# Gate operands by pairs of tokens, and one product for eight tokens, in a one-core two-block kernel

## The chip, the cores and the metric

The kernel runs on one core of one Trainium2 chip, in one launch. The metric is device time in microseconds (us): the time of one execution on the chip. The time before is the median of three runs.

## What is computed

The reference is a model of two blocks on 256 tokens of width 1024. The first mixes three branches (a gated linear recurrence, a stick-breaking attention and an attention to a memory) and ends in a convolved feed-forward layer. The second mixes an attention with another recurrence and ends in a layer of 16384 experts. Only this last layer concerns the change:

```python
s = jnp.einsum('thcd,hcnd->thcn', qp, subkeys)        # 8 heads, 2 x 128 keys
v1, i1 = lax.top_k(s[:, :, 0], 16)
v2, i2 = lax.top_k(s[:, :, 1], 16)
...                                                   # the best 16 of the 16 x 16 sums, per head
eidx = jnp.take_along_axis(cidx, p, axis=-1)          # expert = i1 * 128 + i2
gates = jax.nn.softmax(sc, axis=-1)
ue, ve = u[eidx], v[eidx]
act = jax.nn.gelu(jnp.einsum('td,thkd->thk', xb, ue), approximate=False)
return jnp.einsum('thk,thkd->td', gates * act, ve)
```

So each token picks 128 experts (8 heads by 16), with a gate each; the output sums gate times gelu(x u) times v over them.

## The kernel before, in words

The kernel gathers nothing. It multiplies all tokens by all 16384 rows of u, takes the gelu, multiplies the result by a dense matrix of gates that is zero where an expert was not picked, and multiplies that by all of v. Expert number i1 * 128 + i2 has i1 on the 128 partitions and i2 along the free axis. The activations are two buffers `act` (A[0] and A[1], one for each half of i2), each 128 partitions by 64 values of i2 by 256 tokens, the token innermost, float32.

**The stages of `peer` (line 1682).** `peer_select` (line 1582) finds the picked experts, with some tiles of the u product between its steps; it leaves four fp16 tiles `ix`: i1, i2, and the gate times 16384 as a high and a low part, 128 slots on the partitions and 256 tokens along the free axis. Then lines 1749 to 1754 write down: the rest of the u product, `gate(0)`, `values(0)`, `gate(1)`, `values(1)`. A tile of the u product is 48 matmuls of 256 columns into PSUM tile `psg` (float32 split into a high and a low part, weights `whi` and `wlo`), then a gelu into `act`. `values` multiplies a half of the activations (again split, tiles `hn`) by v into four PSUM tiles `out`, 24 matmuls of 512 columns for each of 32 steps. For both products ScalarE makes `whi` and VectorE makes `wlo` of each load `wraw`.

**`gate(half)` (line 1697)** takes eight tokens at a time (G = 8), 32 times. VectorE compares i1 with 0 to 127 into `oa` (line 1707), i2 with this half's 64 values into `ob` (line 1710), and multiplies `ob` by the two parts of the gate into `oc` (line 1713). All three are fp16 with four tokens innermost; `iof` (line 1685) holds each of 0 to 127 four times, so that both operands are read in runs of four. Then, for each of two groups of four tokens, TensorE multiplies each token's `oa` (128 slots by 128 values of i1, the weights) by its `oc` (128 slots by 2 x 64, the moving operand) into a quarter of a PSUM tile `g` (line 1718). Both operands are read with a step of four elements, 8 bytes. The 128 columns of a token are the high and the low part of the gates of 64 experts. ScalarE takes the low part into `gs` (line 1723), VectorE adds the high part to it (line 1724, here the sum), and VectorE multiplies the four tokens' columns of the activations by it (line 1726, here the product). In PSUM and in `gs` the 64 experts are innermost, in `act` the tokens; the product reads `gs` with the token as its inner index, one float every 256 bytes.

**What orders the work.** The kernel writes its operations into a list, and a planner (`Program.run`, line 347) replays them with costs of its own (line 560 for matmuls: 0.061 us for a g matmul; line 594 for VectorE) and puts them in the order of their planned starts, on all engines. A buffer of a tag is free again when its last use has ended in this replay. In this part TensorE takes the ready matmul with the longest work behind it. So the interleaving of g with psg and out is fixed when the kernel is built, and each engine follows its own fixed list. The tags here are `oa`, `ob`, `oc` with two buffers each (lines 1841 to 1843) and `gs` with three (line 1844); two PSUM tiles are left for `g`. Every instruction is issued from line 514, which is why the profile's rows all name it; the tiles tell them apart.

Of the kernel before, what the change touches and what calls it, by code (L numbers as in the profile page):

```python
# [12 lines left out]
F16 = mybir.dt.float16  # L13
U32 = mybir.dt.uint32
AF = mybir.ActivationFunctionType
ALU = mybir.AluOpType
# [3 lines left out]
P = 128  # L20
T = 256
# [130 lines left out]
class View:  # L152
# [15 lines left out]
    v = rearrange  # L168
# [348 lines left out]
class Kernel:  # L517
# [67 lines left out]
    def act(self, out, in_, func=AF.Copy, bias=None, scale=None, accum_out=None):  # L585
        kw = {}
        for k, x in (("bias", bias), ("scale", scale), ("accum_out", accum_out)):
            if x is not None:
                kw[k] = x
        cost = 0.094 + out.n * 0.83e-3 + 0.093 * sum(isinstance(x, View) for x in (bias, scale))  # L590
        o = self.pr.op("ACT", "activation", (out, in_, func), kw, [in_, bias, scale], [out, accum_out], cost)
        o.table = TABLE.get(func)
# [1089 lines left out]
    def peer(self, outs, H, Q0):  # L1682
        pr, act = self.pr, self.act
        hh, hl = self.ktiles(H[:2]), self.ktiles(H[2:])
        iof = pr.buf("iof", 4 * P, F16)
        self.copy(iof.rearrange("p (n t) -> p n t", t=4),
                  self.iota.rearrange("p (n u) -> p n u", u=1).to_broadcast([P, P, 4]))
        A = [pr.buf("act", 64 * T) for _ in range(2)]

        def done(i, ps):  # L1690
            if i == 0:
                self.first_u = ps
            act(A[i // 32][:, (i % 32) * 512:(i % 32) * 512 + 512], ps, AF.Gelu)

        ix = self.peer_select(hh, hl, A[1], Q0, lambda i, j: self.gemm_t("u", range(i, j), hh, hl, done))

        def gate(half):
            a3 = A[half].rearrange("p (n t) -> p n t", t=T)
            G = 8
            for q in range(T // G):  # L1700
                ts_ = slice(q * G, q * G + G)

                tok = lambda v, n: v[:, ts_].rearrange("p (g u t) -> p g u t", u=1, t=4).to_broadcast([P, 2, n, 4])
                four = lambda o: o.rearrange("p (g n t) -> p g n t", g=2, t=4)
                rep = lambda v: v.rearrange("p (u n t) -> p u n t", u=1, t=4)
                oa = pr.buf("oa", G * P, F16)
                self.tt(four(oa), tok(ix[0], P), rep(iof).to_broadcast([P, 2, P, 4]), ALU.is_equal)

                eq, hl = pr.buf("ob", G * 64, F16), pr.buf("oc", G * P, F16)
                self.tt(four(eq), tok(ix[1], 64), rep(iof[:, half * 256:half * 256 + 256]).to_broadcast([P, 2, 64, 4]),  # L1710
                        ALU.is_equal)
                for n in range(2):
                    self.mul(four(hl[:, n * G * 64:(n + 1) * G * 64]), four(eq), tok(ix[2 + n], 64))
                oa3, hl3 = four(oa), hl.rearrange("p (u g n t) -> p u g n t", u=2, g=2, t=4)
                for g in range(2):
                    ps = self.ps("g")
                    for t in range(4):
                        self.mm(ps[:, t * P:(t + 1) * P].rearrange("p (u n) -> p u n", u=2), oa3[:, g, :, t],
                                hl3[:, :, g, :, t])
                    pv = ps.rearrange("p (t u n) -> p u t n", t=4, u=2)  # L1720
                    sm = pr.buf("gs", T)
                    s3 = sm.rearrange("p (t n) -> p t n", t=4)
                    act(s3, pv[:, 1], scale=1.0 / 16384)
                    self.stt(s3, pv[:, 0], 1.0 / 16384, s3, ALU.mult, ALU.add)
                    av = a3[:, :, q * G + g * 4:q * G + g * 4 + 4]
                    self.mul(av, av, sm.rearrange("p (t n) -> p n t", t=4))

        def values(half):
            for i in range(half * 32, half * 32 + 32):
                vs = self.weights("v", i)  # L1730
                hl = pr.buf("hn", 1024, F32R)
                hi, lo = hl[:, :512], hl[:, 512:]
                self.split(A[half][:, (i % 32) * 512:(i % 32) * 512 + 512], hi, lo)
                order = [(j, tb, hf) for j in range(2) for tb in range(2) for hf in range(2)]
                for j, tb, hf in order if i < 63 else sorted(order, key=lambda x: x[1:]):
                    wh, wl = vs[j]
                    s = slice(j * T + tb * P, j * T + tb * P + P)
                    last = i == 63 and j == 1
                    o = outs[tb * 2 + hf]
                    w = slice(hf * 512, hf * 512 + 512)  # L1740
                    for n, (l, r) in enumerate(((hi, wh), (hi, wl), (lo, wh))):
                        self.mm(o, l[:, s], r[:, w], False, last and n == 2, skip=True)
                if i == 62:

                    ss = self.small(1)
                    o = self.pr.op("ACT", "activation", (ss, self.eps, AF.Sqrt), {}, [self.eps, hi], [ss], 0.1)
                    o.table = TABLE[AF.Sqrt]

        self.gemm_t("u", range(24, 32), hh, hl, done)
        self.gemm_t("u", range(32, 64), hh, hl, done)  # L1750
        gate(0)
        values(0)
        gate(1)
        values(1)

        gb = A[0][:, 0:1024]
        self.load(gb, self.a["normf_g"].partition_broadcast(P))
        sq = A[0][:, 3072:3584]
        for tb in range(2):
            ss, y = self.small(2), A[0][:, (tb + 1) * 1024:(tb + 2) * 1024]  # L1760
            hs = [slice(half * 512, half * 512 + 512) for half in range(2)]
            for half, h in enumerate(hs):
                act(sq, outs[tb * 2 + half], AF.Square, accum_out=ss[:, half:half + 1])
            self.add(ss[:, 0:1], ss[:, 0:1], ss[:, 1:2])
            act(ss[:, 0:1], ss[:, 0:1], AF.Sqrt, scale=1.0 / 1024, bias=self.eps)
            for half, h in enumerate(hs):
                self.mul(y[:, h], outs[tb * 2 + half], gb[:, h])
            self.recip(ss[:, 0:1], ss[:, 0:1])
            act(y[:, hs[0]], y[:, hs[0]], scale=ss[:, 0:1])
            self.ts(y[:, hs[1]], y[:, hs[1]], ss[:, 0:1], ALU.mult)  # L1770
            for h in hs:
                self.store(self.o["out"][tb * P:(tb + 1) * P, h], y[:, h])
# [6 lines left out]
    def run(self):  # L1779
# [3 lines left out]
        with ExitStack() as ctx:  # L1783
# [42 lines left out]
            with tc.tile_pool(name="ap", bufs=1) as ap:  # L1826
                for name, n in (("act", 2), ("ix", 4), ("iof", 1), ("oa", NOA), ("ob", NOB), ("oc", NOC), ("gs", NGS)):
                    pr.tag(name, ap, n)
# [12 lines left out]
NOA = 2  # L1841
NOB = 2
NOC = 2
NGS = 3
NQ0 = 2
RE = (0, 0, 0, 0, 0)
NEARLY = 1
# [99 lines left out]
```

## Time and profile before

| | us |
|---|---|
| median of 3 runs | 1532.84 |
| lowest, highest | 1531.59, 1533.38 |
| the profiled execution | 1533.29 |
| its span, first to last instruction | 1531.5 |

The profile is of one execution. Its span is 1.8 us shorter than its time; the rest lies around the first and the last instruction. A busy time is the union of an engine's records; a record's length includes the way through the engine, so records of one engine overlap, and the distance from one start to the next is what an instruction costs in a row of them. Loads of weights into TensorE have an engine of their own (PEld), since they overlap the matmuls (PE). The first block ends near 545 us (the last matmul of its feed-forward layer on gh starts at 544.9), the product w_q begins at 686.9, the last step of the choice of experts (tile ig) ends by 941.3, and from there to the end run the rest of the u product, the gates and the v product.

### The profile page before, as it was taken

To read this page: it belongs to the slowest core of one execution; us is meant where nothing else is said; L and a number is where in the kernel's file an instruction comes from. 1 tells how busy PE (TensorE), PEld (TensorE's weight loads), DVE (VectorE), ACT (ScalarE), POOL (GpSimd) and SP (SyncE) were. 2 spreads that over 40 slices of the span, in tenths; PEclk is the share of its full clock that TensorE was granted. 3 is DMA by queue.
4 is the path that set the end of the run, shared out by engine and by line. 5 is a ranking of instruction groups with operands and counts; after the bars stand their busy time and mean duration, and the time that the engine had idled before them with its cause. 6 is when DMAs were issued, how large, how long until landed. Compare 5 with 4: busy or idle time off the path is not lost.

```text
span 1531.5 us, 28738 instructions
## 1 busy us (share of the span) xinstructions
PE 1507.1 (98%) x11828; PEld 1384.5 (90%) x11828; DVE 1206.9 (79%) x2214; ACT 821.3 (54%) x1169; POOL 41.0 (3%) x52
## 2 busy tenths in 40 slices
PE   7999999999999999999999999999999999999998
PEld 7888889999999999799999999999997777788886
DVE  7895585678888569767977899999969999955554
ACT  5663575446666465664444446555555555544444
POOL 0010000000123000000000000000000000000000
PEclk9999999999999999999999999999999999999999
DMA  6432124555455553334454555343454444455553
GB/s 234 163 111 85 61 79 138 193 195 184 175 191 187 174 207 119 138 122 182 168 191 175 184 174 185 140 163 138 163 179 169 161 160 157 159 193 192 191 192 135
DMA packets 38436, 249.09 MB, mean 163 GB/s; under 512 B 4000, under 2 KB 7456, under 8 KB 9504
## 3 DMA queue, kind: packets, MB, share of 16 engines
q1 hardware_dynamic: 38304, 247.26, 45.2%
q8 instruction: 92, 1.51, 0.4%
q14 instruction: 40, 0.33, 0.1%
HBM read 246.19 MB, written 1.05 MB: 161 GB/s over the span
## 4 chain that ended last, share of the span: by engine, by line
PE 92%; DVE 4%; ACT 2%; DMA 1%; issue 1%; SPq 0%; ACTq 0%; DVEq 0%
PE psg L514 57%; PE out L514 22%; PE ps L514 8%; PE g L514 4%; DVE wlo L514 2%; ACT whi L514 1%; PE sc L514 0%; DMA wraw<-in_w_rwkv 0%; DMA wraw<-in_w_up 0%; DVE tmp L514 0%; ACT mo L514 0%; ACT L514 0%; DVE gate L514 0%; PE hs L514 0%; ACT act L514 0%
## 5 line engine op out<-in xcount | busy, mean ns | idle before, releaser
L514 ACT ACTIVATE whi<-wraw 128x1024 fp32r<-128x1024 f32 (+1 forms) x458 | 482.3, 1055 | 526.3 <-PE psg L514 336.0
L514 DVE TENSOR_TENSOR wlo<-wraw,whi 128x1024 fp32r<-128x1024 f32 (+1 forms) x458 | 559.7, 1225 | 233.9 <-ACT whi L514 231.1
L514 PE MATMUL psg<-hn,whi 128*128 128x256 f32 x3808 | 692.8, 284 | 10.3 <-ACT whi L514 8.9
L514 PEld LDWEIGHTS psg<-hn,whi 128*128 128x128 f32 x3808 | 589.9, 190 | 11.4 <-ACT whi L514 8.9
L514 PE MATMUL psg<-hn,wlo 128*128 128x256 f32 x1904 | 538.1, 283 | 1.3 <-DVE wlo L514 1.3
L514 PEld LDWEIGHTS psg<-hn,wlo 128*128 128x128 f32 x1904 | 360.5, 189 | 2.2 <-DVE wlo L514 2.2
L514 PE MATMUL out<-whi,hn 128*128 128x512 f32 x1024 | 332.0, 396 | 0.0
L514 PEld LDWEIGHTS out<-whi,hn 128*128 128x128 f32 x1024 | 193.4, 189 | 40.4
L514 PE MATMUL out<-wlo,hn 128*128 128x512 f32 x512 | 200.7, 392 | 0.0
L514 PEld LDWEIGHTS out<-wlo,hn 128*128 128x128 f32 x512 | 96.6, 189 | 18.5
L514 ACT ACTIVATE gs<-g 128x256 f32<-128x256 f32 x128 | 49.1, 383 | 73.8 <-PE g L514 53.2
L514 PE MATMUL g<-oc,oa 128*128 128x128 f16 x512 | 80.2, 295 | 0.2 <-DVE gs L514 0.2
L514 DVE TENSOR_TENSOR act<-act,gs 128x256 f32<-128x256 f32 x128 | 80.0, 626 | 0.0
L514 PE MATMUL psg<-whi,hn 128*128 128x512 f32 x224 | 77.2, 405 | 0.3 <-ACT rg L514 0.3
L514 PEld LDWEIGHTS <-oa 128*128 128x128 f16 x512 | 45.6, 120 | 18.9 <-DVE act L514 7.7
L514 DVE SCALAR_TENSOR_TENSOR gs<-g,gs 128x256 f32<-128x256 f32 x128 | 53.8, 420 | 0.1
L514 PEld LDWEIGHTS psg<-whi,hn 128*128 128x128 f32 x224 | 42.1, 188 | 11.2 <-issue 1.2
L514 DVE TENSOR_TENSOR oc<-ob,ix 128x512 f16<-128x512 f16 x128 | 50.3, 421 | 0.0
L514 PE MATMUL psg<-gh,wlo 128*128 128x256 f32 x176 | 49.7, 283 | 0.6 <-DVE wlo L514 0.6
L514 PE MATMUL psg<-gl,whi 128*128 128x256 f32 x176 | 49.6, 282 | 0.0
L514 PE MATMUL psg<-gh,whi 128*128 128x256 f32 x176 | 49.5, 281 | 0.0
L514 PE MATMUL psg<-yh,wlo 128*128 128x256 f32 x160 | 45.2, 282 | 0.0
(319 smaller groups left out, 1756.2 us busy)
## 6 DMA issues: line engine op xcount, KB each, us to landing
wraw<-in_u SPq DMA_DIRECT2D x64, 1024.0 KB, 4.8
wraw<-in_v SPq DMA_DIRECT2D x64, 1024.0 KB, 4.8
wraw<-in_w_up SPq DMA_DIRECT2D x22, 1024.0 KB, 4.8
wraw<-in_w_gate SPq DMA_DIRECT2D x12, 1024.0 KB, 4.8
wraw<-in_w_out SPq DMA_DIRECT2D x8, 1024.0 KB, 5.0
wraw<-in_w_down SPq DMA_DIRECT2D x8, 1024.0 KB, 4.8
wraw<-in_w_q SPq DMA_DIRECT2D x8, 1024.0 KB, 4.9
wraw<-in_w_rwkv SPq DMA_DIRECT2D x6, 1024.0 KB, 4.9
```

The costliest lines, as they stand in the source:

```text
L514: getattr(eng[e], method)(*[lower(x) for x in args], **{k: lower(x) for k, x in kw.items()})
```

## The change

Tokens lie two by two innermost in the fp16 operands: `iof` holds each number twice, the views of `oa`, `ob` and `oc` have four groups of two tokens, and a matmul reads its operands with a step of two elements. `gs` becomes a buffer of 64 experts by eight tokens, the token innermost. The activation and the sum of each group of four tokens read PSUM with the token as the inner index, one float every 512 bytes, and write their four tokens' columns of that buffer. One product of 512 elements for eight tokens follows both groups, with `gs` read in its own order. `gs` has two buffers in place of three.

```diff
-        iof = pr.buf("iof", 4 * P, F16)
-        self.copy(iof.rearrange("p (n t) -> p n t", t=4),
-                  self.iota.rearrange("p (n u) -> p n u", u=1).to_broadcast([P, P, 4]))
+        iof = pr.buf("iof", 2 * P, F16)
+        self.copy(iof.rearrange("p (n t) -> p n t", t=2),
+                  self.iota.rearrange("p (n u) -> p n u", u=1).to_broadcast([P, P, 2]))
...
-                tok = lambda v, n: v[:, ts_].rearrange("p (g u t) -> p g u t", u=1, t=4).to_broadcast([P, 2, n, 4])
-                four = lambda o: o.rearrange("p (g n t) -> p g n t", g=2, t=4)
-                rep = lambda v: v.rearrange("p (u n t) -> p u n t", u=1, t=4)
+                tok = lambda v, n: v[:, ts_].rearrange("p (g u t) -> p g u t", u=1, t=2).to_broadcast([P, 4, n, 2])
+                four = lambda o: o.rearrange("p (g n t) -> p g n t", g=4, t=2)
+                rep = lambda v: v.rearrange("p (u n t) -> p u n t", u=1, t=2)
                 oa = pr.buf("oa", G * P, F16)
-                self.tt(four(oa), tok(ix[0], P), rep(iof).to_broadcast([P, 2, P, 4]), ALU.is_equal)
+                self.tt(four(oa), tok(ix[0], P), rep(iof).to_broadcast([P, 4, P, 2]), ALU.is_equal)
...
-                oa3, hl3 = four(oa), hl.rearrange("p (u g n t) -> p u g n t", u=2, g=2, t=4)
+                oa3, hl3 = four(oa), hl.rearrange("p (u g n t) -> p u g n t", u=2, g=4, t=2)
+                sm = pr.buf("gs", G * 64).rearrange("p (n t) -> p n t", t=G)
                 for g in range(2):
                     ps = self.ps("g")
                     for t in range(4):
-                        self.mm(ps[:, t * P:(t + 1) * P].rearrange("p (u n) -> p u n", u=2), oa3[:, g, :, t],
-                                hl3[:, :, g, :, t])
-                    pv = ps.rearrange("p (t u n) -> p u t n", t=4, u=2)
-                    sm = pr.buf("gs", T)
-                    s3 = sm.rearrange("p (t n) -> p t n", t=4)
-                    act(s3, pv[:, 1], scale=1.0 / 16384)
-                    self.stt(s3, pv[:, 0], 1.0 / 16384, s3, ALU.mult, ALU.add)
-                    av = a3[:, :, q * G + g * 4:q * G + g * 4 + 4]
-                    self.mul(av, av, sm.rearrange("p (t n) -> p n t", t=4))
+                        j = g * 4 + t
+                        self.mm(ps[:, t * P:(t + 1) * P].rearrange("p (u n) -> p u n", u=2), oa3[:, j // 2, :, j % 2],
+                                hl3[:, :, j // 2, :, j % 2])
+                    pv = ps.rearrange("p (t u n) -> p u n t", t=4, u=2)
+                    s4 = sm[:, :, g * 4:g * 4 + 4]
+                    act(s4, pv[:, 1], scale=1.0 / 16384)
+                    self.stt(s4, pv[:, 0], 1.0 / 16384, s4, ALU.mult, ALU.add)
+                self.mul(a3[:, :, ts_], a3[:, :, ts_], sm)
...
-NGS = 3
+NGS = 2
```

The comparison into `ob` changes in the same way as the one into `oa`.

## Rows read from the trace of the kernel before

**Rows 1.** The page: TensorE's busy time with its share of the span and its instructions, and the chain that ended last, by engine.

```profile
PE 1507.1 (98%) x11828; PEld 1384.5 (90%) x11828; DVE 1206.9 (79%) x2214; ACT 821.3 (54%) x1169; POOL 41.0 (3%) x52
PE 92%; DVE 4%; ACT 2%; DMA 1%; issue 1%; SPq 0%; ACTq 0%; DVEq 0%
```

**Rows 2.** Busy time by stretch: the stretch in us, its length, then busy us and number of instructions of PE, PEld, DVE, ACT and POOL, the granted TensorE clock, the DMA engines' busy share and GB/s.

```profile
946.70:1106.20 159.50, 159.50 (x1342) 156.75 (x1341) 157.45 (x294) 82.09 (x132) 0.00 (x0) 1.00 0.42 152
1106.20:1143.90 37.70, 37.70 (x320) 37.50 (x319) 24.50 (x37) 18.10 (x24) 0.00 (x0) 1.00 0.48 168
1143.90:1331.40 187.50, 187.34 (x927) 147.11 (x925) 183.40 (x319) 99.89 (x149) 0.00 (x0) 1.00 0.46 166
1331.40:1531.50 200.10, 193.60 (x849) 158.58 (x847) 109.64 (x117) 95.26 (x116) 0.00 (x0) 0.99 0.50 179
```

**Rows 3.** The same stretches for the instructions that write or read tile g alone: PE (the g matmuls), PEld, DVE (the sums), ACT.

```profile
946.70:1106.20 159.50, 39.51 (x256) 0.00 (x0) 26.50 (x63) 24.20 (x64) 1.00 0.42 152
1106.20:1143.90 37.70, 3.03 (x20) 0.00 (x0) 1.69 (x4) 1.41 (x4) 1.00 0.48 168
1143.90:1331.40 187.50, 36.98 (x232) 0.00 (x0) 24.73 (x59) 23.00 (x60) 1.00 0.46 166
1331.40:1531.50 200.10, 0.64 (x4) 0.00 (x0) 0.83 (x2) 0.45 (x2) 0.99 0.50 179
```

**Rows 4.** The last stretch for tile out: PE (matmuls, two of them begun before the stretch), PEld (their weight loads), DVE, ACT.

```profile
1331.40:1531.50 200.10, 193.37 (x845) 158.23 (x843) 2.77 (x4) 2.72 (x8) 0.99 0.50 179
```

**Rows 5.** The timeline of PE around one group of g in the u stretch: start, us from the first start to the last end of the merged instructions, engine, line, operation, out<-in, shape, count.

```profile
954.40 0.64 PE L514 MATMUL g<-oc,oa 128*128 128x128 f16 x4
954.79 0.49 PE L514 MATMUL psg<-hn,whi 128*128 128x256 f32 x2
955.12 0.28 PE L514 MATMUL psg<-hn,wlo 128*128 128x256 f32 x1
955.24 0.40 PE L514 MATMUL psg<-hn,whi 128*128 128x256 f32 x2
955.48 0.28 PE L514 MATMUL psg<-hn,wlo 128*128 128x256 f32 x1
```

**Rows 6.** The timeline of PEld at the same group, the weight loads of g.

```profile
954.40 0.35 PEld L514 LDWEIGHTS <-oa 128*128 128x128 f16 x4
```

**Rows 7.** The timeline of PE around one group of g in the v stretch.

```profile
1201.52 0.64 PE L514 MATMUL g<-oc,oa 128*128 128x128 f16 x4
1201.91 0.48 PE L514 MATMUL out<-whi,hn 128*128 128x512 f32 x1
1202.23 0.39 PE L514 MATMUL out<-wlo,hn 128*128 128x512 f32 x1
1202.45 0.63 PE L514 MATMUL out<-whi,hn 128*128 128x512 f32 x2
1202.92 0.39 PE L514 MATMUL out<-wlo,hn 128*128 128x512 f32 x1
```

**Rows 8.** The timeline of DVE in the v stretch: a sum, a product and the split of weights behind it.

```profile
1206.44 0.42 DVE L514 SCALAR_TENSOR_TENSOR gs<-g,gs 128x256 f32<-128x256 f32 x1
1206.78 0.63 DVE L514 TENSOR_TENSOR act<-act,gs 128x256 f32<-128x256 f32 x1
1207.32 1.22 DVE L514 TENSOR_TENSOR wlo<-wraw,whi 128x1024 fp32r<-128x1024 f32 x1
```

**Rows 9.** Groups of instructions of DVE, and one of ACT, by operation, tiles and shape: out<-in, shapes, count | busy us, mean ns of one | idle us before, what ended it.

```profile
L514 DVE TENSOR_TENSOR act<-act,gs 128x256 f32<-128x256 f32 x128 | 80.0, 626 | 0.0
L514 DVE SCALAR_TENSOR_TENSOR gs<-g,gs 128x256 f32<-128x256 f32 x128 | 53.8, 420 | 0.1
L514 DVE TENSOR_TENSOR act<-act 128x256 f32<-128x256 f32 x48 | 18.0, 420 | 0.0
L514 DVE TENSOR_TENSOR hn<-act,hn 128x512 fp32r<-128x512 f32 x64 | 43.7, 685 | 0.0
L514 DVE TENSOR_TENSOR kt<-dd,rq 128x512 f32<-128x512 f32 x3 | 2.1, 697 | 0.0
L514 DVE TENSOR_TENSOR oc<-ob,ix 128x512 f16<-128x512 f16 x128 | 50.3, 421 | 0.0
L514 DVE TENSOR_TENSOR oa<-ix,iof 128x1024 f16<-128x1024 f16 x64 | 44.0, 687 | 0.0
L514 ACT ACTIVATE gs<-g 128x256 f32<-128x256 f32 x128 | 49.1, 383 | 73.8 <-PE g L514 53.2 <-DVE act L514 18.9 <-DVE wlo L514 1.1
```

**Rows 10.** The page's costliest groups, matmuls and weight loads, with the same columns.

```profile
L514 PE MATMUL psg<-hn,whi 128*128 128x256 f32 x3808 | 692.8, 284 | 10.3 <-ACT whi L514 8.9
L514 PE MATMUL g<-oc,oa 128*128 128x128 f16 x512 | 80.2, 295 | 0.2 <-DVE gs L514 0.2
L514 PEld LDWEIGHTS psg<-hn,whi 128*128 128x128 f32 x3808 | 589.9, 190 | 11.4 <-ACT whi L514 8.9
L514 PEld LDWEIGHTS <-oa 128*128 128x128 f16 x512 | 45.6, 120 | 18.9 <-DVE act L514 7.7
```

**Rows 11.** Who waited for whom from 946 to 1335 us: the waiting instruction, what ended the wait, us in all, times, the longest.

```profile
ACT gs L514 <- PE g L514: 53.2, 91, 1.4
ACT gs L514 <- DVE act L514: 18.9, 17, 1.9
```

More of the change, by code (lines that the diff above doesn't have):

```diff
@@ L1701, in gate @@
                 ts_ = slice(q * G, q * G + G)
-                tok = lambda v, n: v[:, ts_].rearrange("p (g u t) -> p g u t", u=1, t=4).to_broadcast([P, 2, n, 4])
-                four = lambda o: o.rearrange("p (g n t) -> p g n t", g=2, t=4)
-                rep = lambda v: v.rearrange("p (u n t) -> p u n t", u=1, t=4)
+                tok = lambda v, n: v[:, ts_].rearrange("p (g u t) -> p g u t", u=1, t=2).to_broadcast([P, 4, n, 2])
+                four = lambda o: o.rearrange("p (g n t) -> p g n t", g=4, t=2)
+                rep = lambda v: v.rearrange("p (u n t) -> p u n t", u=1, t=2)
                 oa = pr.buf("oa", G * P, F16)
-                self.tt(four(oa), tok(ix[0], P), rep(iof).to_broadcast([P, 2, P, 4]), ALU.is_equal)
+                self.tt(four(oa), tok(ix[0], P), rep(iof).to_broadcast([P, 4, P, 2]), ALU.is_equal)
                 eq, hl = pr.buf("ob", G * 64, F16), pr.buf("oc", G * P, F16)
-                self.tt(four(eq), tok(ix[1], 64), rep(iof[:, half * 256:half * 256 + 256]).to_broadcast([P, 2, 64, 4]),
+                self.tt(four(eq), tok(ix[1], 64), rep(iof[:, half * P:half * P + P]).to_broadcast([P, 4, 64, 2]),
                         ALU.is_equal)
```

## The prediction

> **What bounds the kernel now.** I read the page's busy times and its chain first, then busy times by stage, then single instructions of the gate stages. TensorE is busy for 98% of the span, and 92% of the chain that ended last lies on it [rows 1]. The granted clock is 1.00 in all the stages that matter, the 2.4 GHz level [rows 2]. So a change pays only where TensorE has less to do, or where another engine begins to hold it up.
>
> The change touches the gate work, the tile g. Its 512 matmuls lie mainly in two stretches [rows 3]: in the first (946.7 to 1106.2 us, half 0) they are strewn among the matmuls of the table u, in the second (1143.9 to 1331.4 us, half 1) among those of v. TensorE is full in both, and VectorE nearly so: 157.45 of 159.50 us and 183.40 of 187.50 us [rows 2]. Between and after them TensorE is full and VectorE has room.
>
> I divide by the work on eight tokens, a portion of eight g matmuls: 256/8 = 32 portions in the first stretch, 232/8 = 29 in the second [rows 3]. A portion takes 159.5/32 = 4.98 us in half 0, with VectorE busy for 4.92 of it, and 187.5/29 = 6.47 us in half 1, with VectorE busy for 6.32. The two engines are within 0.06 and 0.15 us of each other: what one saves counts only as far as the other follows. At the end of half 1, 843 matmuls of v are left (by their weight loads [rows 4]), where the second half alone has 768; so the gate work is 75 matmuls early, 17 us at 0.23 us each.
>
> **TensorE's part.** In the u stretch the three psg matmuls from 955.12 to 955.48 us take 0.12 us each. Four g matmuls and two of psg lie from 954.40 to 955.12, so the four take 0.72 - 0.24 = 0.48 us, 0.12 each [rows 5]. In the v stretch four g and one out take 0.71 us from 1201.52 on, and an out takes 0.23: again 0.48 [rows 7]. A g matmul streams 128 columns, one of psg 256, one of out 512. From 256 to 512 columns the price goes from 0.12 to 0.23 us, 0.43 ns a column; 128 columns should take 0.12 - 0.055 = **0.065 us**. The g matmuls cost almost twice that, the price of 256 columns, and their records are longer too (295 ns against 284 [rows 10]). What sets them apart is the step: their fp16 operands are read every 8 bytes, those of psg and out every 4. The change makes it 4. The bounds are thus 0.065 and 0.120 us. I take 0.065: the rows with a step of 4 bytes stream at that rate and hide a weight load of 128 columns behind every matmul, though their load records are the longer ones (190 ns against 120 [rows 10]). That takes 8 x 0.055 = 0.44 us off a portion, so TensorE would need 4.54 us in half 0 and 6.03 in half 1.
>
> The counts of matmuls and weight loads stay, and so do the bytes of the DMAs; no DMA is moved.
>
> **VectorE's part.** Consecutive instructions overlap, so I take start to start: 0.34 us for a sum (record 420 ns), 0.54 us for a product with the activations (626 ns) [rows 8, 9].
>
> - The product: two of 256 elements go (1.08 us), one of 512 comes. A plain product of 256 takes 420 ns; the present one takes 206 more [rows 9]. It reads runs of four activations and, as second operand, one float of gs every 256 bytes. Products on stepped runs in an earlier part (kt<-dd,rq: runs of 16, 4 and 1 floats) show 697 ns for 512 elements, hardly over the 685 of contiguous ones (hn<-act,hn) [rows 9]; so I blame gs, which becomes contiguous. Bounds: 685 ns, or 685 + 412 = 1097 with the surcharge kept on all 512 elements. I take 690, start to start 0.60. Saved: 0.48 us.
> - The sums (two a portion) now read PSUM one float every 512 bytes, where before they read runs of 64. No row shows such a read. The stepped SBUF read above is nearest by its step (+206 ns), the present sum by its memory (+0). I take the middle, +103 ns, and keep both ends. A gain I exclude: the sum's 420 ns are what a plain SBUF product of 256 pays [rows 9]. Added: 0.21 us.
> - The fp16 preparation (ob, oa, two oc) has the same elements in runs of two in place of four. 512 fp16 elements take 421 ns, 512 fp32 ones 685 [rows 9], so two go at a time, and two is what a run still holds. I take no change; at one at a time ob, oc and oa would cost 0.27 x 3 + 0.54 = 1.3 us more a portion.
> - The copy that makes iof halves, once, long before the gates: nothing.
>
> VectorE has 0.48 - 0.21 = 0.27 us less to do: 4.65 us a portion in half 0, 6.05 in half 1. At the ends of the sum's price it is 4.44 and 5.84, or 4.86 and 6.26.
>
> **ScalarE and buffers.** The activation that begins each sum reads the same PSUM shape in 383 ns [rows 9]; the same surcharge (0 to 206 ns) adds at most 0.41 us a portion. ScalarE is busy 82.09 of 159.50 and 99.89 of 187.50 us [rows 2], which covers it; without that cover it would hold the sums in VectorE's queue for as long. It waits 53.2 us for g and 18.9 for act [rows 11]. The sums of eight tokens now wait in one buffer for a later product, but two buffers hold sixteen tokens where three held twelve, so the wait on act should shrink. Behind the product in VectorE's queue stands the split of the next weights, wlo, which TensorE needs next; it moves by 0.1 us at most.
>
> **The sum.** TensorE needs 4.54 and 6.03 us, VectorE 4.65 and 6.05. VectorE would set the pace, and since it never was fuller than 98.7%, I add 1%: 4.70 and 6.11. Half 0: (4.98 - 4.70) x 32 = 9.0 us. Half 1: (6.47 - 6.11) x 29 = 10.4 us. The 24 g matmuls outside [rows 3]: 1.3 us. Less 1 us for what the planner may lose in a new order: **19.7 us**. The profiled execution took 1533.3 us, 0.45 above the median of the runs; 1533.3 - 19.7 = 1513.6, **1514 us**. At the sum's lower end TensorE paces and all 0.44 us count: 14.1 + 12.8 + 1.3 = 28.2 us, 1505. At its upper end VectorE needs 4.91 and 6.32: 2.2 + 4.4 + 1.3 = 7.9 us, 1525.
>
> **Rivals.**
>
> *The g matmuls stay at 0.12 us.* The f32 weight load hides behind a matmul of 0.12; the g load need not hide behind one of 0.065. If a load of 0.055 us and a stream of 0.065 go one after the other, that is 0.12 with any step. For it: the four loads of a group follow one another without a break, 0.35 us from 954.40 on [rows 6]. Against it: no other matmul in these rows works in such turns. VectorE's savings are then hidden: 1533 us, within 3. The Trainium skill speaks for this one. Its page "TensorE: Matmul & The Clock Gate", section "LDWEIGHTS (loading the stationary operand)", counts a load by its columns, P/1.2 ns, 107 ns for 128; and "SBUF — State Buffer", section "Door 1: The DMA port swizzle", asks for two hits on each 16-byte line, which a step of 8 bytes already gives. By these rules the step would not matter and the time would stay; the load record of 120 ns agrees with the first, the 190 ns of as many f32 columns does not.
>
> *VectorE sets a slower pace: slower than before.* Its place is the sums' PSUM read. If one float per 512 bytes takes twice the time per element, a sum goes from 420 to the 685 ns of 512 elements, +0.53 us a portion; and if the product's surcharge comes from the activations' runs, 1 KB apart, and not from gs, it takes 1097 ns, 1.01 start to start, and saves only 0.07. VectorE: +0.46, 5.38 and 6.78 us; (5.38 - 4.98) x 32 + (6.78 - 6.47) x 29 = 12.8 + 9.0 = 22 us more, 1555. It decides once both sums' surcharges and the product come to over 1.08 + 0.06 = 1.14 us; then no faster matmul helps. The kt rows speak against the product's half; nothing speaks for or against the sums'. The skill's "PSUM — Partial Sum Buffer", section "Specifications (TRN2)", has lines of 8 bytes and says that non-contiguous patterns slow matmuls; no row here shows what they do to a reader.
>
> *In between*: the stream gets faster but the load shows, 0.09 us a matmul. TensorE: 4.74 and 6.23 us; 7.7 + 7.0 + 0.7 = 15 us less, 1518.
>
> **How the numbers follow.** Matmuls at the new price and VectorE within its bounds: 0.50 (1505 to 1526). In between: 0.08. Matmuls unchanged: 0.26 (1530 to 1536). VectorE slower: 0.16 (1537 to 1555; a small surcharge is likelier than both large ones). So faster by over 0.2% (3 us, about what a measurement of this kernel can tell from no change) has 0.58, within it 0.26, slower 0.16. The range from 1503 to 1538 leaves out most of the slow case and a little below.
>
> **What the new profile would show.** Right: g matmuls 60 to 70 ns apart; a product of 512 elements near 690 ns; sums between 420 and 626 ns; VectorE at 99% in both stretches if they are dear, TensorE full if not. Wrong: g still 0.12 us apart (then 1533), or products over 1 us or sums over 690 ns with TensorE waiting for VectorE's oc or gs (then above 1537).

## The result, and the profile after

The changed kernel takes **1507.62 us** (median of 4 runs, 1506.92 to 1508.46); the kernel before takes 1533.11 beside it (4 runs). The ratio is 0.9835, interval 0.9823 to 0.9847: 25.5 us less. The forecast was 1514, 6.4 us too slow. The profiled execution took 1508.46 us, with a span of 1506.7.

The page's busy time and its chain by engine, which answer to [rows 1]:

```profile
PE 1482.4 (98%) x11828; PEld 1361.0 (90%) x11828; DVE 1176.2 (78%) x2150; ACT 813.0 (54%) x1169; POOL 41.0 (3%) x52
PE 93%; DVE 4%; ACT 2%; issue 1%; DMA 1%; SPq 0%; DVEq 0%; ACTq 0%
```

TensorE is still the engine that the end hangs on; it has 24.7 us less to do, almost the whole gain. The stages, which answer to [rows 2] (PE, PEld, DVE, ACT, POOL, granted clock, DMA share, GB/s); they now end at the last g matmul of the u stretch (280 of the 512 are done by then), the end of the u product, the last g matmul of all, and the span's end:

```profile
947.50:1105.50 158.00, 158.00 (x1454) 156.23 (x1454) 155.35 (x290) 86.31 (x142) 0.00 (x0) 1.00 0.46 166
1105.50:1129.90 24.40, 24.40 (x210) 24.40 (x209) 11.12 (x10) 11.57 (x14) 0.00 (x0) 1.00 0.49 173
1129.90:1310.50 180.60, 180.60 (x942) 139.77 (x941) 170.62 (x290) 95.13 (x150) 0.00 (x0) 1.00 0.49 177
1310.50:1506.70 196.20, 189.67 (x832) 155.41 (x829) 107.20 (x112) 93.92 (x114) 0.00 (x0) 0.99 0.49 178
```

TensorE is full in both gate stretches, at the same granted clock of 1.00. VectorE, forecast as the new bound at 99%, stands at 98.3% (155.35 of 158.00) and 94.5% (170.62 of 180.60). The last psg matmul starts at 1129.87 us instead of 1143.76: 13.9 us of the gain lie ahead of it, the rest behind it.

Now TensorE's timeline around a group of g in the u and in the v stretch, as in [rows 5, 7] (start, us, instruction, count):

```profile
1105.35 0.28 PE L514 MATMUL psg<-hn,wlo 128*128 128x256 f32 x1
1105.47 0.40 PE L514 MATMUL g<-oc,oa 128*128 128x128 f16 x4
1105.68 0.48 PE L514 MATMUL psg<-hn,whi 128*128 128x256 f32 x2
1106.00 0.28 PE L514 MATMUL psg<-hn,wlo 128*128 128x256 f32 x1
...
1310.32 0.40 PE L514 MATMUL g<-oc,oa 128*128 128x128 f16 x4
1310.53 0.47 PE L514 MATMUL out<-whi,hn 128*128 128x512 f32 x1
1310.85 0.40 PE L514 MATMUL out<-wlo,hn 128*128 128x512 f32 x1
```

Four g matmuls and two of psg take 0.53 us, where they took 0.72: less 0.24 for psg, 0.29 are left for the four. In the v stretch it is 0.53 less 0.23, 0.30. Within the group the matmuls are quicker: from the first start to the last end there are 0.40 us, less one record of 0.22, so three steps of 0.06 (start to start the median is 58 ns, where it was 118). The fourth step gains far less. From the start of a group's last g matmul to the second f32 matmul behind it the median over the trace is 0.228 us with psg and 0.341 with out, where it was 0.251 and 0.364: 0.023 us less, not 0.060. The second out comes 0.32 us after the first, as it did before [rows 7]; a last g matmul of 58 ns fills less of that time than one of 118. TensorE's weight loads at the same place, and the one behind [rows 6] in the kernel before, show what may be late:

```profile
954.75 0.32 PEld L514 LDWEIGHTS psg<-hn,whi 128*128 128x128 f32 x2
...
1105.47 0.23 PEld L514 LDWEIGHTS <-oa 128*128 128x128 f16 x4
1105.66 0.30 PEld L514 LDWEIGHTS psg<-hn,whi 128*128 128x128 f32 x2
```

The loads of g follow 0.04 to 0.05 us apart and hide. The f32 load behind them, whose record is 190 ns, begins only with the last g matmul (1105.66 us), as it did before (954.75), and has 58 ns to hide under in place of 118. I read the 70 to 80 ns that a group costs beside its matmuls as mainly such a load; no experiment takes the load away, so this cause is argued. That the cost goes with the number of groups is borne out by experiments 7 and 11.

The groups that answer to [rows 9, 10] (busy us, mean ns of one | idle before, what ended it):

```profile
L514 PEld LDWEIGHTS psg<-hn,whi 128*128 128x128 f32 x3808 | 588.9, 190 | 11.7 <-ACT whi L514 9.2 <-DVE hn L514 1.4 <-ACT small L514 0.5
L514 DVE SCALAR_TENSOR_TENSOR gs<-g,gs 128x256 f32<-128x256 f32 x128 | 51.2, 416 | 0.0
L514 DVE TENSOR_TENSOR oc<-ob,ix 128x512 f16<-128x512 f16 x128 | 48.5, 418 | 0.0
L514 PE MATMUL g<-oc,oa 128*128 128x128 f16 x512 | 46.6, 221 | 0.0
L514 DVE TENSOR_TENSOR oa<-ix,iof 128x1024 f16<-128x1024 f16 x64 | 44.0, 687 | 8.4 <-PE g L514 8.4
L514 ACT ACTIVATE gs<-g 128x256 f32<-128x256 f32 x128 | 43.9, 376 | 17.1 <-PE g L514 15.7 <-DVE act L514 1.0
L514 DVE TENSOR_TENSOR act<-act,gs 128x512 f32<-128x512 f32 x64 | 43.7, 684 | 0.1
L514 PEld LDWEIGHTS <-oa 128*128 128x128 f16 x512 | 29.7, 98 | 17.2 <-issue 13.8 <-DVE act L514 0.8 <-DVE gs L514 0.8
```

One product of 512 takes 684 ns for two of 626. The sums, which now read PSUM one float every 512 bytes, take 416 ns for 420, and the activation 376 for 383. The fp16 preparation is unchanged (418 and 687). And VectorE now has idle time ahead of oa, 8.4 us "<-PE g": it waits for TensorE, not the other way round. The waits of ScalarE, from 946 to 1315 us, answer to [rows 11]:

```profile
ACT gs L514 <- PE g L514: 15.7, 30, 0.9
ACT gs L514 <- DVE act L514: 1.0, 3, 0.6
```

An account of the whole gate work: from the first g matmul to the third matmul behind the last one, 385.75 us passed before and 363.63 after. In this time lie 1380 psg matmuls, and 695 of out before, 710 after. Less 0.1189 us for each psg and 0.2297 for each out, their usual distances from start to start, 62.0 us are left for 512 g matmuls before, 121 ns each, and 36.5 after, 71 ns each. The difference is 25.5 us, as much as lies between the medians; the two profiled executions are 24.8 us apart, and in the second the first g matmul starts 0.7 us later.

### The profile page after: what moved, and what is told of

It reads as the page before. It is cut to its first block, busy times and chain, and to the rows that moved or that the text cites. A ratio compares the mean times of both kernels' runs of the same rounds, so it can differ in the third digit from the quotient of the medians.

```text
span 1506.7 us, 28537 instructions
## 1 busy us (share of the span) xinstructions
PE 1482.4 (98%) x11828; PEld 1361.0 (90%) x11828; DVE 1176.2 (78%) x2150; ACT 813.0 (54%) x1169; POOL 41.0 (3%) x52
## 4 chain that ended last, share of the span: by engine, by line
PE 93%; DVE 4%; ACT 2%; issue 1%; DMA 1%; SPq 0%; DVEq 0%; ACTq 0%
PE psg L514 59%; PE out L514 23%; PE ps L514 8%; PE g L514 2%; DVE wlo L514 1%; ACT whi L514 1%; DMA x<-in_xT 1%; PE sc L514 0%; ACT mo L514 0%; ACT L514 0%; DVE tmp L514 0%; DVE gate L514 0%; PE hs L514 0%; ACT act L514 0%; DVE lf L514 0%
## 5 line engine op out<-in xcount | busy, mean ns | idle before, releaser
L514 ACT ACTIVATE gs<-g 128x256 f32<-128x256 f32 x128 | 43.9, 376 | 17.1 <-PE g L514 15.7
L514 DVE TENSOR_TENSOR oa<-ix,iof 128x1024 f16<-128x1024 f16 x64 | 44.0, 687 | 8.4 <-PE g L514 8.4
L514 PE MATMUL g<-oc,oa 128*128 128x128 f16 x512 | 46.6, 221 | 0.0
L514 PEld LDWEIGHTS <-oa 128*128 128x128 f16 x512 | 29.7, 98 | 17.2 <-issue 13.8
```

Source lines behind the costliest of these rows:

```text
L514: getattr(eng[e], method)(*[lower(x) for x in args], **{k: lower(x) for k, x in kw.items()})
```

## The experiments

The kernel before ran beside each set, at 1533.4 to 1533.5 us; the changed kernel itself, run again in the last set, took 1508.26 (1507.70 to 1508.60), ratio 0.9838 (0.9824 to 0.9851). The code is shown as a difference to the changed kernel, in experiment 2 to the kernel before; `...` stands for lines left out.

> The changed kernel itself, to compare with the one with pieces of eight on the same chip: 1506 to 1509 us.

**1. The pairs alone**: the fp16 operands of the change, with the sums, the products and the three gs buffers of the kernel before.

```diff
-                    pv = ps.rearrange("p (t u n) -> p u n t", t=4, u=2)
+                    pv = ps.rearrange("p (t u n) -> p u t n", t=4, u=2)
+                    sm = pr.buf("gs", T)
...
-                self.mul(a3[:, :, ts_], a3[:, :, ts_], sm)
+                    av = a3[:, :, q * G + g * 4:q * G + g * 4 + 4]
+                    self.mul(av, av, sm.rearrange("p (t n) -> p n t", t=4))
```

> Pairs of tokens in the fp16 operands, but sums and products as before (four tokens each, three gs buffers). Theory (TensorE and VectorE share the bound): g matmuls 58 to 60 ns apart as with the whole change, but VectorE keeps its 4.92 and 6.32 us a portion and now sets the pace; the products stay at 626 ns and TensorE begins to wait for VectorE. Gain 4 to 8 us, 1525 to 1529 us. Rival (TensorE alone bounds the gate stretches, VectorE's savings are hidden): the whole gain, 1508 us.

Measured: 1521.41 us, ratio 0.9925 (0.9908 to 0.9941): 12 us of the 25, more than the 4 to 8 that were expected, and not the rival's whole gain. The g matmuls are 58 ns apart, as in the change. Its busy time in the u and in the v stretch, and then its waits from 940 us on:

```profile
945.50:1106.00 160.50, 155.25 (x1392) 150.81 (x1391) 160.50 (x303) 83.83 (x135) 0.00 (x0) 1.00 0.44 157
1137.70:1318.50 180.80, 180.19 (x930) 137.10 (x930) 180.29 (x319) 99.53 (x149) 0.00 (x0) 1.00 0.48 172
```

```profile
PEld L514 <- DVE gs L514: 18.2, 53, 0.8
PE g L514 <- DVE gs L514: 6.1, 17, 0.6
```

VectorE is busy 160.50 of 160.50 us in the u stretch, TensorE 155.25; in the v stretch VectorE has 180.29 of 180.80, and matmuls and loads of g wait for the sums. With faster matmuls VectorE does become the bound, unless it too gets less to do. Part of what came above the expected gain is idle time that VectorE gave up: 4.1 us of 187.5 in the v stretch before [rows 2], 0.5 of 180.8 here.

**2. The sums and the product alone**: the operands stay four by four, the rest is the change's.

```diff
+                sm = pr.buf("gs", G * 64).rearrange("p (n t) -> p n t", t=G)
...
+                    pv = ps.rearrange("p (t u n) -> p u n t", t=4, u=2)
+                    s4 = sm[:, :, g * 4:g * 4 + 4]
...
+                self.mul(a3[:, :, ts_], a3[:, :, ts_], sm)
```

> Operands by fours as before, but the sums of eight tokens in one buffer and one product of 512 elements. Theory: VectorE saves 0.48 us a portion, which is hidden behind g matmuls of 0.12 us: 1531 to 1534 us, products at 684 ns, VectorE 90 to 93% busy in the gate stretches. Rival (VectorE alone bounds them): 10 us or more below before.

Measured: 1532.86 us, ratio 0.9996 (0.9987 to 1.0006). Busy time from 1144 to 1332 us:

```profile
1144.00:1332.00 188.00, 188.00 (x929) 148.11 (x927) 169.34 (x288) 93.39 (x147) 0.00 (x0) 1.00 0.46 168
```

VectorE has 14 us less to do in this stretch than in [rows 2] (169.34 against 183.40), and no time is saved: TensorE is full. So 12 us and 0.6 us (no change, by its interval), one at a time, make 25 together. The pairs alone make VectorE the bound; the sums and the product alone relieve an engine that is not the bound.

**3 and 4. Which operand's step?** Pairs in the weights (`oa`) only, and pairs in the stream (`ob`, `oc`) only.

```diff
+        TA, TM = 2, 4        # experiment 4: TA, TM = 4, 2
...
-                        self.mm(..., oa3[:, j // 2, :, j % 2], hl3[:, :, j // 2, :, j % 2])
+                        self.mm(..., oa3[:, j // TA, :, j % TA], hl3[:, :, j // TM, :, j % TM])
```

> The changed kernel, but only oa (the weights of the g matmuls) lies by pairs; ob and oc (the moving operand) lie by fours, read every 8 bytes. Theory (the stream of the moving operand runs at half rate with a step of 8 bytes): g stays 116 to 118 ns apart, 1531 to 1534 us. Rival (the weight load is what the step slows): g 58 to 65 ns apart, 1508 us. If both count, between 75 and 105 ns, 1515 to 1527 us.

> The reverse: oc, the moving operand, by pairs, oa, the weights, by fours. Theory (stream): g 58 to 65 ns apart, 1508 us. Rival (weight load): g 116 to 118 ns apart, 1531 to 1534 us. If both count, between 75 and 105 ns, 1515 to 1527 us.

Measured: 1530.99 us, ratio 0.9983 (0.9974 to 0.9993), with pairs in the weights; 1510.11 us, 0.9848 (0.9832 to 0.9865), with pairs in the stream: g 116 and 60 ns apart, the theory of the stream in both. A group of g in the timeline of the first, then of the second:

```profile
1180.82 0.63 PE L514 MATMUL g<-oc,oa 128*128 128x128 f16 x4
1181.20 0.48 PE L514 MATMUL out<-whi,hn 128*128 128x512 f32 x1
1181.52 0.39 PE L514 MATMUL out<-wlo,hn 128*128 128x512 f32 x1
```

```profile
1180.45 0.43 PE L514 MATMUL g<-oc,oa 128*128 128x128 f16 x4
1180.69 0.48 PE L514 MATMUL out<-whi,hn 128*128 128x512 f32 x1
1181.01 0.39 PE L514 MATMUL out<-wlo,hn 128*128 128x512 f32 x1
```

Less an out of 0.23, four take 0.47 us in the first and 0.33 in the second, against 0.30 in the change. It is the step of the stream that sets the price; that of the weights adds some 2 us in all.

**5 and 6. The step further up and down**: tokens by eights in both operands (16 bytes), and singly (2 bytes, contiguous).

```diff
-                four = lambda o: o.rearrange("p (g n t) -> p g n t", g=4, t=2)
+                four = lambda o: o.rearrange("p (g n t) -> p g n t", g=1, t=8)    # 6: g=8, t=1
```

`iof` and the other views follow in the same way.

> The changed kernel with eight tokens innermost: a matmul reads its operands every 16 bytes. Theory (the stream takes 8 bytes of one partition at a time: one column at a step of 8 bytes, two at a step of 4): 16 bytes is no worse than 8, g 116 to 120 ns apart, 1531 to 1534 us. Rival (the rate goes on falling with the step): g about 220 ns apart, 512 x 0.1 = 52 us more, about 1585 us.

> One token innermost: a matmul reads contiguous operands, and VectorE's token operand stands still in a row of 64 or 128. Theory: g no faster than at a step of 4 bytes, 56 to 60 ns apart; VectorE falls to one fp16 element at a time (oa 1220 ns, ob and oc 685 ns), 1.3 us more a portion, and sets the pace: 1570 to 1585 us. Rival (contiguous operands stream faster still, and VectorE keeps two elements at a time): below 1508 us.

Measured with eights: 1594.84 us, ratio 1.0402 (1.0385 to 1.0419). My theory, that a step of 16 bytes is no worse than 8, fell; the rival, that the price goes on rising with the step, stands. Its timeline:

```profile
1185.23 2.08 PE L514 MATMUL g<-oc,oa 128*128 128x128 f16 x8
```

Eight in 2.08 us, less a record of 0.41, are seven steps of 0.24 (median 235 ns). Singly: 1576.10 us, 1.0280 (1.0260 to 1.0301). The matmuls are 56 ns apart, hardly faster than pairs, but VectorE pays. Two of its groups, and then the longest of TensorE's waits:

```profile
L514 DVE TENSOR_TENSOR oc<-ob,ix 128x512 f16<-128x512 f16 x128 | 82.1, 678 | 0.0
L514 DVE TENSOR_TENSOR oa<-ix,iof 128x1024 f16<-128x1024 f16 x64 | 77.5, 1211 | 0.2 <-PE g L514 0.2
```

```profile
PE g L514 <- DVE gs L514: 54.5, 58, 2.6
```

With runs of one, VectorE's fp16 work takes 678 and 1211 ns for 418 and 687, as if two elements no longer went at a time, and TensorE waits 54.5 us. A run of two is the one length here at which both engines are quick.

**7 and 8. What cheapened the product?** The change with two products of 256 and three gs buffers, but the token innermost in `gs`; and the change with its one product of 512, but `gs` with the expert innermost, so that the product reads it every 256 bytes.

```diff
# 7
+                    s4 = pr.buf("gs", T).rearrange("p (n t) -> p n t", t=4)
...
+                    av = a3[:, :, q * G + g * 4:q * G + g * 4 + 4]
+                    self.mul(av, av, s4)
# 8
+                sm = pr.buf("gs", G * 64).rearrange("p (t n) -> p t n", t=G)
...
+                self.mul(a3[:, :, ts_], a3[:, :, ts_], sm.rearrange("p t n -> p n t"))
```

> Pairs of tokens, the sums written with the token innermost as in the change, but each group of four tokens in its own buffer (three of them) with its own product of 256. Theory (the old product's surcharge came from the step of gs): product 420 ns, 0.07 us more a portion than one product of 512, TensorE still sets the pace: 1507 to 1511 us. Rival (it came from the activations' short runs): product 626 ns, and the time of pairs alone, 1521 us.

> Pairs of tokens and one product of 512 elements, but gs keeps the expert innermost, so that PSUM is read in runs of 64 as before and the product reads one float of gs every 256 bytes. Theory: the surcharge stays on every element, product 1050 to 1150 ns, VectorE sets the pace as with pairs alone: 1516 to 1522 us. Rival (the surcharge went with the longer runs of activations): product 684 ns, 1508 us.

Measured: 1509.80 us, ratio 0.9847 (0.9831 to 0.9864), and 1520.57 us, 0.9921 (0.9904 to 0.9938). The product in either:

```profile
L514 DVE TENSOR_TENSOR act<-act,gs 128x256 f32<-128x256 f32 x128 | 52.8, 414 | 0.0
```

```profile
L514 DVE TENSOR_TENSOR act<-act,gs 128x512 f32<-128x512 f32 x64 | 70.6, 1105 | 0.0
```

The surcharge is gs's step: without it 256 elements cost 414 ns, with it 512 cost 1105. The order of gs is worth 12 us. One product in two buffers of eight tokens, instead of two in three of four, is worth about 2 us (1509.8 against 1507.6 and 1508.3). This is not VectorE's price: in the seventh kernel TensorE is busy for 159.00 of 159.00 us from 947 us on, and for 178.00 of 178.00 from 1130 us on. The account used above leaves 38.0 us for its g matmuls, where the change has 36.5, and its plan has them in 117 groups, where the change has 98 (neighbouring groups of four count as one): 1.5 us for 19 groups, 0.08 each. In the eighth kernel TensorE waits for gs as in the first (7.2 us, and its loads 13.1).

**9 and 10. The weights by eights, the stream by pairs; and the reverse**: `TA, TM = 8, 2` and `2, 8` in the edit of 3.

> The changed kernel with oa (the weights) by eights, read every 16 bytes, and oc (the moving operand) by pairs. Theory (the step of the moving operand alone sets the pace of the stream): g 58 to 75 ns apart, 1507 to 1513 us. Rival (the weight load, 97 ns a record by pairs and 146 by eights, is half of what eights cost): g 110 to 150 ns apart, 1530 us or more.

> The reverse: oa by pairs, oc by eights. Theory: g 230 to 240 ns apart, as with both by eights, 1590 to 1596 us. Rival: g 150 to 200 ns apart, 1555 to 1580 us.

Measured: 1516.58 us, ratio 0.9891 (0.9873 to 0.9910), and 1589.11 us, 1.0365 (1.0346 to 1.0383). The first fell between the theory and its rival, the second 1 us below the theory (229 ns apart). The loads and matmuls of a group in the first:

```profile
1182.08 0.34 PEld L514 LDWEIGHTS <-oa 128*128 128x128 f16 x4 [0.26 <-issue]
```

```profile
1182.08 0.47 PE L514 MATMUL g<-oc,oa 128*128 128x128 f16 x4
```

A load's record is 149 ns, over 98 in the change. In the middle of a group the matmuls are 64 ns apart, but the first step of a group takes about 120 ns (71 in the change): the load shows mainly once a group, 8 us in all. The stream by eights alone gives the whole loss of experiment 5 but 6 us.

**11. Groups of eight**: all eight g matmuls in one piece of the plan, to halve the number of times that the f32 load shows.

```diff
+                pss = [self.ps("g") for _ in range(2)]
+                pr.join = True
                 for g in range(2):
-                    ps = self.ps("g")
...
+                pr.join = False
+                for g in range(2):
+                    pv = pss[g].rearrange("p (t u n) -> p u n t", t=4, u=2)
```

> The changed kernel with the eight g matmuls of a portion as one piece of TensorE's order, in two PSUM tiles, in place of two pieces of four. Theory (each return from g to f32 matmuls leaves some 60 ns of a weight load uncovered, 0.29 us for four g in place of 0.23): about 40 returns fewer, 2 to 3 us less than the change, 1504.5 to 1506 us. Rival (with both PSUM tiles taken at once TensorE waits for VectorE's sums): 1508 us or more, with waits of PE g for DVE gs.

Measured: 1515.68 us, ratio 0.9888 (0.9872 to 0.9903), 7 to 8 us slower than the change. The theory's time did not come, the rival's did, with its waits of PE g for DVE gs (6.6 us). They have one place, between the halves:

```profile
1124.68 0.63 PE L514 MATMUL g<-oc,oa 128*128 128x128 f16 x8
1128.23 0.39 PE L514 MATMUL g<-oc,oa 128*128 128x128 f16 x4 [2.92 <-DVE gs L514]
...
1133.44 0.59 PE L514 MATMUL g<-oc,oa 128*128 128x128 f16 x4 [1.28 <-DVE gs L514]
1134.44 0.58 PE L514 MATMUL g<-oc,oa 128*128 128x128 f16 x4 [0.42 <-DVE gs L514]
1136.04 0.80 PE L514 MATMUL out<-whi,hn 128*128 128x512 f32 x1 [1.01 <-ACT hn L514]
1136.63 0.63 PE L514 MATMUL out<-wlo,hn 128*128 128x512 f32 x1
```

```profile
1124.00:1136.00 12.00, 4.43 (x40) 3.27 (x38) 11.80 (x26) 4.28 (x10) 0.00 (x0) 0.74 0.25 89
1136.00:1141.00 5.00, 4.96 (x17) 3.78 (x18) 4.86 (x10) 2.13 (x6) 0.00 (x0) 0.61 0.32 105
1129.90:1139.90 10.00, 6.21 (x25) 4.63 (x25) 9.91 (x24) 3.50 (x8) 0.00 (x0) 0.50 0.15 47
```

The plan spread the larger pieces wider, and at 1124.6 us all psg matmuls were done, with 32 g matmuls still ahead of the first of out in TensorE's order. Nothing lay between these to cover VectorE's work, and TensorE was busy 4.43 of 12 us. From 1129.9 to 1139.9 us the granted clock was 0.50, the level of 1.2 GHz, and out matmuls came 427 ns apart. From 1124.68 to the next group at 1140.70 us, 16.0 us went for 32 g and 12 out. The 12 take 2.8 us at their usual price, so 13.3 us went for 32 g matmuls worth 2.1.

Outside that place the account used above gives 65.7 ns for a g matmul, where the change has 71.2. A group of eight thus costs 526 ns, and one of the change's, 5.2 matmuls on average, 372. If each matmul has one price and each group another on top, the two equations give about 55 ns for a matmul and 80 for a group, an estimate. By it the theory's gain is there (5.5 ns x 512 = 2.8 us), and the schedule lost more. Why the plan spread the pieces that way was not tried.

## Why the prediction came out as it did

*What bounds the kernel.* Right: TensorE, before and after; VectorE just behind it.

*The g matmuls.* The mechanism was right: the step of the operand, 4 bytes for 8, not the weight load, sets the price (experiments 3 to 5, 9, 10). The size was near: 0.065 us was forecast; it is 0.058 from start to start, and some 0.07 on top for every group, 0.071 on average. The sum priced every g matmul by its columns alone and had no term for what stands behind a group. 512 x 0.006 = 3 us are about what separates the sum's lower end (28.2 us) from the 25.5 measured. The 1 us taken off for the planner is not found: the account puts all 25.5 us on the g matmuls.

*The sums: the step that failed.* "I take the middle, +103 ns" for PSUM reads of one float every 512 bytes. They cost nothing: 416 ns and 376 ns. (The lines of 8 bytes in the Trainium skill's "PSUM — Partial Sum Buffer", "Specifications (TRN2)", made no difference to these two readers.) Without that term VectorE has the price at the lower end of its bounds (4.44 and 5.84 us a portion), below TensorE's, and "VectorE would set the pace" fell with it, the 1% added for that pace too. With this one term VectorE set the forecast's pace, at 19.7 us of gain; without it the sum is that of its lower end, 28.2. The forecast still came within 6.4 us because the term moves the bound by little: VectorE's price with it (4.65 and 6.05 us) lies close above TensorE's (4.54 and 6.03).

*The product.* Right: 690 ns forecast, 684 measured, and gs's step was to blame (7 and 8).

*The fp16 preparation at no cost.* Right, and no matter of course: singly it costs 1576 us (6).

*Buffers.* Right: ScalarE's wait for act went from 18.9 to 1.0 us; with three buffers of four tokens and the cheap products it was still 16.4 us (7).

*The rivals.* "The g matmuls stay at 0.12": refuted by 3 and 4; with the weights still by fours and the stream by pairs they are 60 ns apart. With it falls what was drawn from the Trainium skill's "SBUF — State Buffer", "Door 1: The DMA port swizzle": a step of 8 bytes gives the two hits on each 16-byte line, yet the stream took 118 ns, against 58 at 4 bytes. The Trainium skill's rule P/1.2 ("TensorE: Matmul & The Clock Gate", "LDWEIGHTS (loading the stationary operand)") gives an estimate of 107 ns, near the load's record of 98 ns, but loads of g follow each other at 58 ns, so they overlap. "In between" (0.09 us, 1518): a part of it came, 0.071 on average, for the f32 load behind a group by the reading above more than for g's own load, whose first step takes 71 ns for 58. "VectorE sets a slower pace": neither of its two prices came (416 and 684 ns), and the change's form avoids the one that exists, 1105 ns in experiment 8.

## What to carry to other kernels

Where two engines are within a few per cent of each other in a stretch, add the two savings and the two bounds together, not one by one: here 12 and 0.6 us apart made 25 together. Read the step of a matmul's streamed operand before its weights': here 4 bytes cost hardly more than 2, and 8 bytes twice as much. Let the layout's run length be one that the engine that writes it still takes at full rate (here two fp16 elements). Where no row prices an access, a middle value can decide which engine the sum names as the bound; state the time on both sides of that switch.

## What the runs showed of the hardware that was not expected

- TensorE's price for 128 fp16 columns against the step of the stream: 56 ns at 2 bytes (6), 58 at 4, 116 at 8 (3), 229 at 16 (10), the last three with the weights by pairs. Up to 4 bytes it is nearly the same, and from there to 16 bytes it doubles with the step.
- The step of the weights costs far less: load records of 98, 117 and 149 ns at 4, 8 and 16 bytes, which show mainly in the first step of a group (71, 88 and 120 ns, with the stream by pairs).
- Behind a group of g the second f32 matmul comes 0.228 us (psg) and 0.341 us (out) after the last g matmul starts, where 0.251 and 0.364 passed with g matmuls of twice the price: little of what the last g matmul saves is gained.
- VectorE and ScalarE read PSUM one float every 512 bytes at no cost (416 and 376 ns, before 420 and 383), while VectorE pays for an SBUF operand read every 256 bytes: 1105 ns for 684 on 512 elements.
- In experiment 11 TensorE was busy for 4.43 of 12 us. Inside that time, from 1129.9 us on, the granted clock fell to 0.50, the level of 1.2 GHz, and stayed there until 1139.9, though TensorE was busy again from 1136 us on; out matmuls came 427 ns apart for 229.
